# A two-layer trunk on one core: the attention's output product in plain fp32, and five places of split weights lent to the experts' weights

## The chip, the cores and the metric

The kernel runs on one core of a Trainium2 chip. The metric is the device time of one execution in microseconds (us), median of several runs. One execution is also profiled; its times are read below.

## The reference

The input is 256 positions of 1024 channels. Layer 0 is a gated short convolution and a dense SwiGLU. Layer 1 is an attention over 15 heads of 64 and a mixture of 8 experts, of which each position takes 2. Cut to what matters here:

```python
def dilated_attention_mixer(h, positions, w_qkv, w_o):
    ...                                    # 3 groups of 5 heads, softmax over the groups too
    return o.reshape(b, s, ATTN_WIDTH) @ w_o          # (256 x 960) @ (960 x 1024)

def moe_swiglu(h, w_router, w_gate, w_up, w_down):
    ...                                    # gates: top 2 of 8, softmax
    for e in range(N_EXPERTS):
        out = out + gates[..., e:e + 1] * swiglu(h, w_gate[e], w_up[e], w_down[e])
```

An expert has three matrices of 1024 x 2816 fp32, 33 MiB together, and the eight have 264 MiB.

## The kernel before

**The stream of weights.** All weights come from HBM through one object, `Stream`, in the order in which `add_*` has listed them. An item is about 1 MiB (here called a unit). The kinds that matter: `"w"`, weights of the dense layers and of the attention, which are split on arrival into a rounded part (`whi`, by ScalarE) and a remainder (`wlo`, by VectorE, L222), each an fp32r tile of the pool `ring` (six of each); `"m"`, rows of `mod_w`, which VectorE adds up at once into `acc_ab` or `acc_g` (L287); `"r"`, raw fp32 weights, which the experts use unsplit. Each load takes a slot from `st.slots`. For `"w"` and `"m"` the slot goes back into the list as soon as the load is listed, and the next load into it waits on SyncE (SP) until the reader has finished; for `"r"` it goes back only at `done()`. SP issues all these loads in the order in which the code listed them. What `topup` lists is decided here:

```python
            kind, more = self.loaded[0][:2] if self.loaded else self.items[0][::2]
            if kind == "r":
                return bool(self.slots)
            n = len(more[1]) if kind == "w" else 0 if kind == "p" else 2
            return n + sum(len(u.tiles) for q in (self.ready, self.held) for u in q if not callable(u)) <= 2 * N_SPLIT
```

With `N_SPLIT = 3`, three units of split weights (six pairs of tiles) may be ready or held; an `"m"` counts as two tiles, a raw unit as none. Listing an `"m"` also puts its two adds into VectorE's program at that place.

**Order around the change.** The QKV products run as six passes (`n` 0 to 5) of two units each (`units[0]` to `units[11]`). The stream's list there is: `units[10]`, `late_g[0]`, `units[11]`, `late_g[1]`, the four units of `w_o`, `late_g[2]`, `late_g[3]`, then the experts' units, expert by expert. The five general slots `raw0` to `raw4` go round. In the last pass the first scores (`scores(its[0])`, `expo`, `norm`) stand before the products of `units[11]`, and ScalarE's copies of `vv` behind `expo`. Attention then runs as a pipeline of turns, one for each of ten pairs of head group and row half: scores, softmax, transposes, `values`. `values` leaves its result in PSUM; ScalarE rounds it into `oT[0]`, VectorE the remainder into `oT[1]` (tiles hTh, hTl).

**The output product.** `out_proj` multiplies with the four units of `w_o`: `rows` issues three fp32r matmuls of 512 columns for every block of 128 channels, row half and column half (xh by wh, xh by wl, xl by wh). One unit goes through both row halves first, with `attention_end` (the last turn) between them; the other three are kept and run by row half and column half, with the router's work (`mid`, `after`) in between. Then come the router, the choice and the gather, and the experts.

**The experts.** Each expert runs over groups of 32 tokens: two groups always, a third if it has more than 64 tokens, a fourth over 96 (`by_groups`). At `e == 1` all engines meet for a test (`overflow`, not taken). Slots for the experts' units beside the five general ones: `acc_ab`, `early0` (once), `tables`, `rawx`, six `ring` places of one pair `whi`, `wlo` each (2 x 512 KB), `rows`, `h`; each is added to the list when its first owner is done.

Of the kernel before, what the change touches and what calls it, by code (L numbers as in the profile page):

```python
# [10 lines left out]
F32 = mybir.dt.float32  # L11
# [3 lines left out]
AF = mybir.ActivationFunctionType  # L15
# [3 lines left out]
P = 128  # L19
D = 1024  # L20
S = 256
NT = S // P
KT = D // P
# [4 lines left out]
HD = 64  # L28
AW = NH * HD
# [12 lines left out]
N_SPLIT = 3  # L42
# [10 lines left out]
def trunk_kernel(ctx: ExitStack, tc: tile.TileContext, a, out):  # L53
    nc = tc.nc
    ve, sc, pe, gp = nc.vector, nc.scalar, nc.tensor, nc.gpsimd

    cst = ctx.enter_context(tc.tile_pool(name="cst", bufs=1))
    pers = ctx.enter_context(tc.tile_pool(name="pers", bufs=1))
    ring = ctx.enter_context(tc.tile_pool(name="ring", bufs=2 * N_SPLIT))
# [3 lines left out]
    def f32(ap):  # L63
        return ap.bitcast(F32)
# [4 lines left out]
    def tp_tile():  # L69
        return psum.tile([P, 512], F32, name="tp", tag="tp", bufs=2)  # L70

    def mm(o, l, r, start, stop):
        pe.matmul(o, l, r, start=start, stop=stop, skip_group_check=True)  # L73
# [64 lines left out]
    def part_of(raw, n, c0, c1):  # L138

        if isinstance(raw, list):  # L140
            h, c1 = c0 // 1024, c1 - c0 // 1024 * 1024
            return raw[h][:n, c0 - h * 1024:c1]
        return raw[:n, c0:c1]
# [127 lines left out]
    st = Stream()  # L271
# [131 lines left out]
    def unit(*args):  # L403
        return lambda: add_unit(*args)
# [4 lines left out]
    def mod_g(n):  # L409
        return [lambda q=q: mods[n].add_g(q) for q in range(4)]  # L410
# [6 lines left out]
    def in_order(*units):  # L417
        for u in units:
            u()
# [41 lines left out]
    w_qkv, w_o = a["attn_w_qkv"][0], a["attn_w_o"][0]  # L461
# [3 lines left out]
    late_g = mod_g(3)  # L465
    plan(units[6:10], mod_ab(3, (1,)))
    in_order(units[10], late_g[0], units[11], late_g[1])
    os = [unit(w_o, 2 * q, 2, 0, D) for q in range(3)]
    in_order(*os)

    def load_last(raw):
        nc.sync.dma_start(part_of(raw, P, 0, D), w_o[6 * P:7 * P, :])
        nc.sync.dma_start(part_of(raw, HD, D, 2 * D), w_o[7 * P:AW, :])
    st.add_w(load_last, D, [(P, 0, D), (HD, D, 2 * D)])
    in_order(*late_g[2:])

    def add_raw(w, k0, nk, c0, cw):

        pad = 1024 if nk == 2 else cw
        half = 1024 // pad  # L480

        def load(raw):
            for f, n in [(0, half), (half, nk - half)] if isinstance(raw, list) else [(0, nk)]:
                dst = part_of(raw, P, f * pad, (f + n) * pad).rearrange("p (k n) -> p k n", n=pad)[:, :, :cw]
                nc.sync.dma_start(dst, w[(k0 + f) * P:(k0 + f + n) * P, c0:c0 + cw].rearrange("(k p) n -> p k n", p=P))
        st.add_r(load, pad)

    for e in range(NE):
        for c0, cw in ROUNDS:
# [36 lines left out]
    def modulated(i, rstd, mod, hs, h=None):  # L526
# [4 lines left out]
        ve.tensor_add(h[:, c], h[:, c], mod.B[:, c])  # L531
        return h

    def split_to(hi, lo, src):
        sc.activation(hi, src, AF.Copy)  # L535
        ve.tensor_sub(lo, src, f32(hi))
# [7 lines left out]
    def new_hT():  # L544
        return (pers.tile([P, KT, S], F32R, name="hTh"), pers.tile([P, KT, S], F32R, name="hTl"))
# [24 lines left out]
    def rows(po, u, xs, first, last, cols=(0, 512)):  # L570

        n = len(xs)
        for kk, (xh, xl) in enumerate(xs):
            r = xh.shape[0]
            for c0 in cols:
                wh, wl = u.at(kk * D + c0, 512, r)
                o = po[c0 // 512]
                mm(o, xh, wh, first and kk == 0, False)
                mm(o, xh, wl, False, False)
                mm(o, xl, wh, False, last and kk == n - 1)  # L580
# [206 lines left out]
    for n in range(3):  # L787
        u = st.get(99 if n else 1)
# [20 lines left out]
    for n in range(3):  # L809
        u = st.get()  # L810
# [6 lines left out]
        if n == 1:  # L817
            t = conv_sum(0, v)
    ps = [mm_tile() for _ in range(3)]
    for n in range(3):  # L820
        for kh in range(2):
            u = st.get()
# [8 lines left out]
            if kh == 1 and n == 1:  # L831
                t = conv_sum(1, v)
# [25 lines left out]
    with tc.tile_pool(name="ffn", bufs=1) as pool:  # L858
# [5 lines left out]
        for n, (c0, cw) in enumerate(PIECES):  # L864
# [3 lines left out]
            for w, k0 in ffn_order(turns) if n == 0 else turns:  # L868
                u = st.get()
# [52 lines left out]
        r = rstd_of(1, lambda: st.finish(1))  # L922
# [9 lines left out]
    oT = None  # L932
# [30 lines left out]

    its = [(j, i) for j in range(HPG) for i in range(NT)]
    Ss, Ps, PTs = {}, {}, {}
    rests = deque()
    scale = HD ** -0.5

    def head(j, g):
        hd = order[g] * HPG + j  # L970
        return hd, slice(HD * (hd % 2), HD * (hd % 2) + HD)
# [41 lines left out]
    def values(it):  # L1013
        j, i = it
        pt = PTs.pop(it)
        n = i + 1
        p = tp_tile().rearrange("p (g t) -> p g t", g=4)
        for g in range(3):
            hd, rs_ = head(j, g)
            for b in range(n):  # L1020
                mm(p[rs_, g], vv[:, b, hd * HD:(hd + 1) * HD], pt[:, g * n + b], b == 0, b == n - 1)
        ts = slice(i * P, (i + 1) * P)
        _, rs_ = head(j, 0)
        b0 = j // 2
        hd, rs2 = head(j, 2)
        parts = ((rs_, slice(b0, b0 + 6, 5), slice(0, 2)), (rs2, hd // 2, 2))
        for r, b, g in parts:
            sc.activation(oT[0][r, b, ts], p[r, g], AF.Copy)

        def rest():  # L1030
            for r, b, g in parts:
                ve.tensor_sub(oT[1][r, b, ts], p[r, g], f32(oT[0][r, b, ts]))
        rests.append(rest)

    for n, (c0, cw) in enumerate(QKV):
        if n == 2:
# [48 lines left out]
        else:  # L1085
            for kh in range(2):
                u = st.get()
# [7 lines left out]
                        post(i)  # L1095
                st.done(0 if n == len(QKV) - 1 and kh == 1 else 99)

    def router_scale(q):
        p = mm_tile().rearrange("p (r k t) -> p r k t", r=2, k=4)
        for r, row in enumerate((mods[3].A, mods[3].B)):  # L1100
            for k in range(4):
                pe.transpose(p[:, r, k], row[:, (4 * q + k) * P:(4 * q + k + 1) * P], ident)
        sc.activation(col_a[:, 4 * q:4 * q + 4], p[:, 0, :, 0], AF.Copy)
        bT.append(pool.tile([P, 4, P], F32, name="bT", tag="rope", bufs=3))
        sc.activation(bT[q], p[:, 1], AF.Copy)
# [7 lines left out]

    bT = []
    N = len(its)
    oT = new_hT()
    def turn(n):
        if n == N:
            sc.activation(warm, eps, AF.Sqrt)
        if 0 < n < N:  # L1120
            scores(its[n])
        if 0 < n - 1 < N:
            norm(its[n - 1])
        while rests:
            rests.popleft()()
        if 0 <= n - 2 < N:
            probs(its[n - 2])
            probs_out(its[n - 2])
        if 0 < n < N:
            expo(its[n])  # L1130
        if n in (9, 10):
            router_scale(n - 9)
        if n == 11:
            st.topup()
        if n == 10:
            st.add_slot("acc_ab", lambda: pers.tile([P, 2048], F32, name="raw", tag="acc_ab"))
        if n == 12:
            router_shift()
        if 0 <= n - 3 < N:
            values(its[n - 3])  # L1140
        if n == N + 2:
            rests.popleft()()

    for n in range(N + 2):
        turn(n)
# [1 line left out]
    def attn_act(q, i):  # L1147
        r = []
        for k in (2 * q, 2 * q + 1):
            m = P if k < 7 else HD  # L1150
            r.append((oT[0][:m, k, i * P:(i + 1) * P], oT[1][:m, k, i * P:(i + 1) * P]))
        return r

    moe = hT32 = lg = pairs = sel = gates = px = None
# [1 line left out]
    def attention_end():  # L1156

        nonlocal moe, hT32, lg, pairs, sel, gates, px
        turn(N + 2)
        attn.close()  # L1160
        moe = ctx.enter_context(tc.tile_pool(name="moe", bufs=1))

        st.add_slot("early0", lambda: moe.tile([P, 2048], F32, name="early0", tag="acts"), once=True)
        st.add_slot("tables", lambda: [pers.tile([P, 1024], F32, name="rawt", tag="tables"),
                                       moe.tile([P, 1024], F32, name="rawm")])
        hT32 = moe.tile([P, KT, S], F32, name="hT32", tag="rawx")
        lg = moe.tile([P, NT, NE], F32, name="lg")
        pairs = moe.tile([P, NT, 2, NE, NE], F32, name="pairs", tag="xg")
        sel = moe.tile([P, NT, NE], BF16, name="sel")
        gates = moe.tile([P, NT, NE], F32, name="gates")  # L1170
        px = moe.tile([P, NT, NE], F32, name="px")
# [74 lines left out]
    def gathered(pr, ks, p, copy):  # L1246
        if pr not in xg:
            xg[pr] = moe.tile([P, KT, S], F32, name="xg", tag="xg")
        copy(xg[pr][:, ks[0]:ks[-1] + 1].rearrange("p k t -> p (k t)"), p[:, :len(ks) * S])

    def act_copy(o, i):
        sc.activation(o, i, AF.Copy)  # L1252

    def spread(e):

# [122 lines left out]
    for_router(1, 1)  # L1378
    router(1, 1, lp)
    st.add_slot("rawx", lambda: moe.tile([P, 2048], F32, name="rawx", tag="rawx"))  # L1380
    for n in range(2 * N_SPLIT):
        st.add_slot(f"ring{n}", lambda: [ring.tile([P, 1024], F32, name="rawr", tag=t) for t in ("whi", "wlo")])
    st.topup()
    rs[1] = rstd_of(1, lambda: remainder_h(0, 0))
    round_h(0, 1)
# [21 lines left out]
    rest = mm_tile()  # L1407
# [15 lines left out]
    for h in range(2):  # L1423
        r = slice(64 * h, 64 * h + 64)
# [100 lines left out]
    _, n_all = nc.values_load_multi_w_load_instructions(counts[0:1, :], engines=[mybir.EngineType.PE], min_val=0, max_val=S)  # L1525
    for e in range(NE):
        pr, b = divmod(e, 2)
# [9 lines left out]
        for r, (c0, cw) in enumerate(ROUNDS):  # L1537
            bank = groups()
            N = cw // 2
# [88 lines left out]
    r = moe.tile([P, NT], F32, name="r")  # L1628
    t = moe.tile([P, NT], F32, name="t")
# [7 lines left out]
    last = cols[-1].start  # L1637
# [35 lines left out]
```

## Time and profile before

| | |
|---|---|
| median of 3 runs | 1189.1 us (1188.94 to 1191.66) |
| the profiled execution's own time | 1189.74 us |
| its span | 1188.1 us, 20567 instructions |
| busy TensorE (PE) / its weight loads (PEld) | 1102.9 / 614.1 us |
| busy VectorE (DVE) / ScalarE (ACT) | 549.9 / 320.3 us |
| bytes read from HBM | 395.45 MB |

Times in the rows are from the span's start. A row of the timeline gives start, duration, engine (SPq is SP issuing a load), line, operation, out<-in, how many were merged, and in brackets the idle time before it and what ended it. L73 is the helper that records every matmul; a plain fp32 product of the source stands as two MATMUL instructions, an fp32r product as one. The granted clock (PEclk) is 1.00 at 2.4 GHz and 0.50 at 1.2 GHz. The ends of matmuls are modelled, so the distance between starts tells more than a duration.

### The profile page before, as it was taken

The numbers are of one execution on the slowest core, as the hardware profiler recorded it, in microseconds if no ns is written. First come the engines' busy times: TensorE is split into PE (matmuls) and PEld (weight loads), VectorE is DVE, ScalarE is ACT, GpSimd is POOL, SyncE is SP. The second block draws the span as 40 slices with busy tenths as digits, with TensorE's granted clock in tenths as the row PEclk, the third lists the DMA queues.
The fourth block names the chain that finished last, engine by engine and source line by source line (L and its number), as shares of the span: only waits on it lengthen the run. The fifth ranks groups of instructions, "written<-read, shape, count | busy, mean of one in ns | idle before, by whom it ended". The sixth has DMA issues, their size and how long they took to land. (4 is left out here: it accounts for less than half of the span.)

```text
span 1188.1 us, 20567 instructions
## 1 busy us (share of the span) xinstructions
PE 1102.9 (93%) x8658; PEld 614.1 (52%) x8658; DVE 549.9 (46%) x863; ACT 320.3 (27%) x517; POOL 29.6 (2%) x45
## 2 busy tenths in 40 slices
PE   5999999999999999997989999999999999998986
PEld 1899699997878776332323233333333333332233
DVE  3599798887789867321312211221221222321224
ACT  3345444454354473310201110110111021110111
POOL 2000110000001000000000000000000000000000
PEclk9999999999999999998999999999999999998999
DMA  9888797887937915999999999999779999999994
GB/s 339 303 311 330 244 330 288 294 293 283 344 103 276 333 47 192 407 406 408 403 408 408 392 406 408 347 394 400 267 298 404 401 383 408 406 405 408 406 372 156
DMA packets 139400, 398.40 MB, mean 335 GB/s; under 512 B 11299, under 2 KB 22331, under 8 KB 139274
## 3 DMA queue, kind: packets, MB, share of 16 engines
q1 hardware_dynamic: 138698, 396.47, 87.7%
q8 instruction: 101, 1.65, 0.6%
q14 instruction: 25, 0.20, 0.0%
q0 software_dynamic: 576, 0.07, 0.0%
HBM read 395.45 MB, written 1.05 MB: 334 GB/s over the span
## 5 line engine op out<-in xcount | busy, mean ns | idle before, releaser
L73 PE MATMUL mm<-raw,xg 128*32 128x512 f32 (+1 forms) x1616 | 245.8, 570 | 19.1 <-DVEq L1531 7.1
L73 PE MATMUL mm<-rawr,xg 128*32 128x512 f32 (+1 forms) x1360 | 166.7, 559 | 9.2 <-PEq L1435 4.1
L222 DVE TENSOR_TENSOR wlo<-raw,whi 128x1024 fp32r<-128x1024 f32 (+2 forms) x130 | 153.8, 1221 | 27.5 <-ACT whi L220 26.6
L220 ACT ACTIVATE whi<-raw 128x1024 fp32r<-128x1024 f32 (+2 forms) x130 | 132.1, 1045 | 117.3 <-PE mm L73 77.6
L1442 DVE TENSOR_TENSOR gu<-gu,mm 64x512 f32<-64x512 f32 (+1 forms) x96 | 62.0, 646 | 217.2 <-ACT gu L1441 216.7
L73 PE MATMUL mm<-hTh,whi 128*128 128x256 f32 x544 | 150.2, 291 | 1.4 <-ACT hTh L535 1.4
L73 PE MATMUL mm<-hTh,wlo 128*128 128x256 f32 x544 | 146.8, 283 | 0.8 <-DVE wlo L222 0.8
L73 PE MATMUL mm<-hTl,whi 128*128 128x256 f32 x544 | 147.2, 284 | 0.0
L73 PEld LDWEIGHTS mm<-raw,xg 128*32 128x32 f32 x1616 | 70.8, 111 | 130.0 <-issue 103.0
L1441 ACT ACTIVATE gu<-mm 64x512 f32<-64x512 f32 (+1 forms) x96 | 51.5, 551 | 306.0 <-PE mm L73 190.5
L73 PEld LDWEIGHTS mm<-rawr,xg 128*32 128x32 f32 x1360 | 53.3, 110 | 102.4 <-issue 84.8
L73 PEld LDWEIGHTS mm<-hTh,whi 128*128 128x128 f32 x544 | 102.7, 196 | 3.9 <-ACT hTh L535 2.1
L73 PEld LDWEIGHTS mm<-hTl,whi 128*128 128x128 f32 x544 | 101.2, 192 | 2.9 <-issue 1.4
L73 PEld LDWEIGHTS mm<-hTh,wlo 128*128 128x128 f32 x544 | 101.2, 192 | 1.0 <-DVE wlo L222 1.0
L73 PE MATMUL mm<-raw,acts 128*32 128x512 f32 (+1 forms) x784 | 86.3, 562 | 10.7 <-DMA raw<-in_moe_w_down_dram 7.7
L73 PE MATMUL mm<-rawr,acts 128*32 128x512 f32 x608 | 73.2, 595 | 3.6 <-PEq L1433 2.0
L1453 DVE COPY acts<-tp 128x256 f32<-128x256 f32 (+1 forms) x48 | 19.2, 400 | 90.1 <-ACT acts L1252 89.8
L73 PEld LDWEIGHTS mm<-raw,acts 128*32 128x32 f32 x784 | 26.1, 109 | 64.3 <-issue 50.7
L287 DVE SCALAR_TENSOR_TENSOR acc_ab<-raw,csil,acc_ab 128x1024 f32<-128x1024 f32 x40 | 51.2, 1281 | 6.1 <-DMA acc_ab<-in_mod_b_dram 5.4
L73 PE MATMUL mm<-whi,hTh 128*128 128x512 f32 (+1 forms) x128 | 50.1, 409 | 0.7 <-ACT hTh L535 0.7
L1499 DVE TENSOR_TENSOR og<-mm,G 128x512 f32<-128x512 f32 x14 | 9.0, 685 | 89.4 <-PEq L1435 51.7
L73 PE MATMUL mm<-rawx,xg 128*32 128x512 f32 (+1 forms) x224 | 47.9, 561 | 0.8 <-PEq L1435 0.5
(268 smaller groups left out, 1328.9 us busy)
## 6 DMA issues: line engine op xcount, KB each, us to landing
raw<-in_moe_w_down_dram SPq DMA_DIRECT2D x36, 1024.0 KB, 12.7
rawr<-in_moe_w_down_dram SPq DMA_DIRECT2D x66, 512.0 KB, 10.0
raw<-in_mod_w_dram SPq DMA_DIRECT2D x64, 512.0 KB, 5.2
raw<-in_moe_w_gate_dram SPq DMA_DIRECT2D x29, 1024.0 KB, 14.2
raw<-in_moe_w_up_dram SPq DMA_DIRECT2D x27, 1024.0 KB, 13.1
rawr<-in_moe_w_up_dram SPq DMA_DIRECT2D x48, 512.0 KB, 10.4
rawr<-in_moe_w_gate_dram SPq DMA_DIRECT2D x48, 512.0 KB, 10.2
raw<-in_mod_w_dram SPq DMA_DIRECT2D x16, 1024.0 KB, 6.4
```

The lines of the kernel that those rows point to most:

```text
L73: pe.matmul(o, l, r, start=start, stop=stop, skip_group_check=True)
L220: sc.activation(hi[:n, :c1 - c0], src, AF.Copy)
L222: ve.tensor_sub(lo_, src, f32(hi)))
L287: ve.scalar_tensor_tensor(acc, w, csil[:, k:k + 1], acc, op0=OP.mult, op1=OP.add)
L1441: sc.activation(a[64:, :N], bank[g][:64, :N], AF.Silu)
L1442: ve.tensor_mul(a[64 * g:64 * g + 64, :N], a[64:, :N], bank[g][64:, :N])
L1453: copy(acts[:, 8 * r:8 * r + 2 * nb, g:g + 32].rearrange("p (j m) t -> p m j t", j=2), v[:, :, n])
L1499: ve.tensor_mul(og[:, g - 1], bank[g], G2)
```

## The change

`w_o` is loaded as raw fp32 (`"r"`) and not split; `oT` is one fp32 tile, copied from PSUM half by ScalarE and half by VectorE; `rows` issues one fp32 matmul in place of three. `late_g[2]` and `late_g[3]` keep their place in the list behind `w_o`. After the QKV passes five ring places become slots, and for each free slot a load is listed without being used yet; the sixth is added in `attention_end`, and the adding of all six after the output product goes.

```diff
     in_order(units[10], late_g[0], units[11], late_g[1])
-    os = [unit(w_o, 2 * q, 2, 0, D) for q in range(3)]
-    in_order(*os)
-
-    def load_last(raw):
-        nc.sync.dma_start(part_of(raw, P, 0, D), w_o[6 * P:7 * P, :])
-        nc.sync.dma_start(part_of(raw, HD, D, 2 * D), w_o[7 * P:AW, :])
-    st.add_w(load_last, D, [(P, 0, D), (HD, D, 2 * D)])
-    in_order(*late_g[2:])
...
+    for q in range(3):
+        add_raw(w_o, 2 * q, 2, 0, D)
+
+    def load_last(raw):
+        nc.sync.dma_start(part_of(raw, P, 0, D), w_o[6 * P:7 * P, :])
+        nc.sync.dma_start(part_of(raw, HD, D, 2 * D), w_o[7 * P:AW, :])
+    st.add_r(load_last, D)
+    in_order(*late_g[2:])
...
             for c0 in cols:
+                if isinstance(u, RawUnit):
+                    mm(po[c0 // 512], xh, u.at(kk, c0, 512)[:r], first and kk == 0, last and kk == n - 1)
+                    continue
...
-        for r, b, g in parts:
-            sc.activation(oT[0][r, b, ts], p[r, g], AF.Copy)
-
-        def rest():
-            for r, b, g in parts:
-                ve.tensor_sub(oT[1][r, b, ts], p[r, g], f32(oT[0][r, b, ts]))
-        rests.append(rest)
+        for copy, (r, b, g) in zip((act_copy, ve.tensor_copy), parts):
+            copy(oT[r, b, ts], p[r, g])
...
+    def add_split_slots(ns):
+        for n in ns:
+            st.add_slot(f"ring{n}", lambda: [ring.tile([P, 1024], F32, name="rawr", tag=t) for t in ("whi", "wlo")])
+
+    add_split_slots(range(2 * N_SPLIT - 1))
+    for _ in range(len(st.slots)):
+        st.load()
...
-    oT = new_hT()
+    oT = pers.tile([P, KT, S], F32, name="oT", tag="hTh")
...
-        while rests:
-            rests.popleft()()
...
-        if n == N + 2:
-            rests.popleft()()
...
-            r.append((oT[0][:m, k, i * P:(i + 1) * P], oT[1][:m, k, i * P:(i + 1) * P]))
+            r.append((oT[:m, k, i * P:(i + 1) * P], None))
...
+        add_split_slots((2 * N_SPLIT - 1,))
...
-    for n in range(2 * N_SPLIT):
-        st.add_slot(f"ring{n}", lambda: [ring.tile([P, 1024], F32, name="rawr", tag=t) for t in ("whi", "wlo")])
```

## Rows read from the trace of the kernel before

**Rows 1.** Stretches: start:end, length, busy by engine (instructions), PEclk, DMA share, GB/s.
```profile
416.00:441.00 25.00, 24.51 (x200) 19.27 (x198) 18.02 (x49) 20.87 (x49) 0.00 (x0) 1.00 0.02 7
455.00:472.00 17.00, 15.70 (x89) 12.23 (x88) 12.37 (x30) 6.91 (x16) 0.00 (x0) 1.00 0.25 96
...
840.00:860.00 20.00, 19.02 (x160) 6.51 (x156) 5.25 (x8) 1.18 (x2) 0.00 (x0) 1.00 0.71 265
...
1080.00:1100.00 20.00, 16.55 (x100) 3.97 (x92) 4.64 (x7) 2.35 (x4) 0.00 (x0) 0.83 1.03 408
```

**Rows 2.** Timeline of DVE: the first work after an expert's last product.
```profile
544.61 1.29 DVE L1499 TENSOR_TENSOR og<-mm,G 128x512 f32<-128x512 f32 x2 [12.40 <-PEq L1433]
...
632.02 1.29 DVE L1499 TENSOR_TENSOR og<-mm,G 128x512 f32<-128x512 f32 x2 [4.09 <-PEq L1433]
...
936.16 1.29 DVE L1499 TENSOR_TENSOR og<-mm,G 128x512 f32<-128x512 f32 x2 [22.51 <-PEq L1435]
...
1007.84 1.29 DVE L1499 TENSOR_TENSOR og<-mm,G 128x512 f32<-128x512 f32 x2 [4.09 <-PEq L1433]
```

**Rows 3.** Timeline of PE where experts 0 and 1 begin (the latter after the meeting).
```profile
481.45 4.06 PE L73 MATMUL mm<-raw,xg 128*32 128x512 f32 x34 [1.24 <-ACT G L1425]
...
551.60 1.07 PE L73 MATMUL mm<-raw,xg 128*32 128x512 f32 x2 [7.14 <-DVEq L1531]
```

**Rows 4.** Stretch of low clock behind that meeting, columns as in the first group.
```profile
551.60:557.50 5.90, 5.90 (x28) 1.38 (x32) 0.00 (x0) 0.00 (x0) 0.00 (x0) 0.50 1.02 409
```

**Rows 5.** Timeline of SP's loads, from the output weights to the experts' ninth unit.
```profile
392.82 4.89 SPq L281 DMA_DIRECT2D raw<-in_attn_w_o_dram  x3
...
401.86 2.64 SPq L359 DMA_DIRECT2D raw<-in_mod_w_dram  x2
408.30 0.37 SPq L485 DMA_DIRECT2D raw<-in_moe_w_gate_dram  x1
...
440.81 0.37 SPq L485 DMA_DIRECT2D raw<-in_moe_w_gate_dram  x1
...
454.70 0.37 SPq L485 DMA_DIRECT2D raw<-in_moe_w_up_dram  x1
472.17 0.37 SPq L485 DMA_DIRECT2D rawx<-in_moe_w_gate_dram  x1
```

**Rows 6.** Timeline of DVE from the add of `late_g[1]` to the first scores.
```profile
399.24 2.60 DVE L287 SCALAR_TENSOR_TENSOR acc_g<-raw,csil,acc_g 128x1024 f32<-128x1024 f32 x2
...
404.02 0.68 DVE L379 SCALAR_TENSOR_TENSOR rows<-tp,gb 128x512 f32<-128x512 f32 x1
...
408.19 0.55 DVE L983 CUSTOM_DVE_ANT_0 s<-mm,tables 128x384 f32<-128x384 f32 x1
```

**Rows 7.** Issue to landing: the load issued at 401.86, at 440.81, all of L359.
```profile
DMA to landing us min/median/max: 8.0/8.0/8.0
...
DMA to landing us min/median/max: 5.2/5.2/5.2
...
DMA to landing us min/median/max: 5.1/6.4/9.0
```

**Rows 8.** Timeline of ACT and PE: what stands behind the first scores.
```profile
409.40 0.52 ACT L1061 ACTIVATE vv<-mm 128x448 f32<-128x448 f32 x1
...
411.55 1.35 PE L73 MATMUL mm<-kT,qT 64*128 64x256 f32 x12
```

**Rows 9.** Timeline of PE: the same twelve `values` instructions at two clocks.
```profile
418.23 1.14 PE L73 MATMUL tp<-pt,vv 128*64 128x128 f32 x12
...
441.56 1.98 PE L73 MATMUL tp<-pt,vv 128*64 128x128 f32 x12 [0.72 <-DVE hTl L1032]
```

**Rows 10.** Timeline of PE: two fp32 products and the next; first and last of 23 fp32r.
```profile
120.10 1.88 PE L73 MATMUL tp<-acc_g,ones 128*128 128x512 f32 x4
121.41 0.79 PE L73 MATMUL mm<-whi,zh 128*128 128x512 f32 x1
...
445.18 0.39 PE L73 MATMUL mm<-wlo,hTh 128*128 128x512 f32 x1
...
450.17 0.39 PE L73 MATMUL mm<-whi,hTl 128*128 128x512 f32 x1
```

More of the change, by code (lines that the diff above doesn't have):

```diff
@@ L532, in modulated, with act_copy @@
         return h
+    def act_copy(o, i):
+        sc.activation(o, i, AF.Copy)
     def split_to(hi, lo, src):
@@ L965, in trunk_kernel @@
     Ss, Ps, PTs = {}, {}, {}
-    rests = deque()
     scale = HD ** -0.5
@@ L1249, in gathered @@
         copy(xg[pr][:, ks[0]:ks[-1] + 1].rearrange("p k t -> p (k t)"), p[:, :len(ks) * S])
-    def act_copy(o, i):
-        sc.activation(o, i, AF.Copy)
     def spread(e):
```

## The prediction, made before the change was run

> **What bounds the kernel now.** I read the page's forty slices first: the DMA runs near 400 GB/s through the experts' half of the span, with two holes ahead of it and one dip inside it. The stretches put numbers on them [rows 1]: 7 GB/s while attention runs, 96 GB/s in the output product, and 265 GB/s at 840 to 860 us (the next 20 us are alike), while late, at 1080 to 1100 us, it is 408 GB/s again. So the experts' half has three parts. Near its end the weights come too slowly and set the end. In the dip the DMA has filled all places and waits for PE to free them, so PE sets the time there. In the first two experts the ends of the experts tell [rows 2]: expert 1 takes 632.02 - 544.61 = 87.4 us, expert 5, with the same two groups and the same gather inside it, 1007.84 - 936.16 = 71.7 us. Of the 15.7 us more, 7.1 are the meeting of the engines [rows 3] and 5.9/2 = 2.95 the half clock behind it [rows 4]; the other 5.7 us are waits for weights. From this follows the rule by which I count: a PE that reaches the dip later by X makes places free later by X, and the full-rate stream behind the dip ends later by X. Weights that come earlier are worth only what they save PE ahead of the dip, at most those 5.7 us.
>
> **How the stream's list runs now.** SP issues the three full units of `w_o` from 392.82, the two `late_g` loads from 401.86, the experts' first unit at 408.30, and then waits until 440.81 for the slot of a `w_o` unit that is split only in turn 11 [rows 5]. Eight experts' units are issued by 454.70, the ninth follows at 472.17, when the output product is over.
>
> **The hold on VectorE.** This is the costly part, and the diff doesn't name it. Now, when `units[9]` is done, `topup` adds `late_g[1]` (the add from 399.24 to 401.84 [rows 6]), lists the first split of `w_o`, and stops, because three split units stand ready. `late_g[2]` and `late_g[3]` are listed long after. With `w_o` raw, its four units count no tiles and are listed at once, taking four of the five slots; `units[10]` and `units[11]` count four tiles, two more are allowed, so `late_g[2]` and `late_g[3]` are listed too, at the same place, both into the one slot left, that of `late_g[1]`. So VectorE's next instructions are their adds, ahead of the row of L379 and of the first scores at 408.19 [rows 6]. The load of `late_g[2]` is issued when the slot is free, at 401.86 as now [rows 5]; the second must wait until the first is added. The landing took 8.0 us for the load issued at 401.86 and 5.2 us for one into an idle queue; L359's lie between 5.1 and 9.0 [rows 7]. I take 8.0 and 5.2: 401.86 + 8.0 = 409.9, add 2.6, 412.5, issue and landing 417.7, add 420.3, L379 0.68, scores 0.55, so the first scores end at 421.5 instead of 408.7. What is queued behind: ScalarE has `expo` and then the copies of `vv`; the first copy now ends at 409.92, 1.18 us after the scores' end, and PE's next scores need the PSUM tile that it frees. They start at 411.55 now [rows 8], and at 421.5 + 1.2 = 422.7 then. Attention is late by 11.2 us. With both landings at 5.1 it is 8.1, with both at 9.0 15.9 us.
>
> The Trainium skill's page "DMA: Bandwidth & Descriptors", section "Anatomy of one DMA — SWDGE (gpsimd) path", fits a load as 2.0 us plus bytes at 436 GB/s, an estimate of 4.4 us for 1 MiB. By it the hold would be 6.7 us and the forecast 4.5 us lower; no load of L359 here was below 5.1 us, so the rows are kept.
>
> PE then has stood idle for some 11 us. After 7.1 us idle [rows 3] it ran 5.9 us at granted 0.50, which is 1.2 GHz [rows 4]. Twelve `values` instructions took 1.14 us at full and 1.98 us at low clock [rows 9], so 0.84/1.98 of 5.9 us, 2.5 us, would be lost; the bounds are 0 and 2.95, and I take 2.0, as not all of a turn is PE's.
>
> **The output product.** 32 places (8 blocks, 2 row halves, 2 column halves) have three fp32r matmuls now. Their starts are (450.17 - 445.18)/22 = 0.227 us apart [rows 10], so 0.680 us a place. An fp32 product of the same shape stands in the trace as two instructions: two products start at 120.10, and the next fp32r matmul, issued at 121.41, shows 0.79 us instead of 0.39, so it got the array at 121.81 [rows 10]. That is 1.71/2 = 0.855 us a product. By the starts alone it would be 1.31/2 = 0.655. The ends are modelled, but the 0.40 us of queueing is in the row, so I take 0.855: 32 x 0.175 = +5.6 us, the other end being -0.8. PE is without a gap in this part and the router behind it starts from the last product, so this is on the path. Nothing comes back from the removed splits of ScalarE and VectorE, since PE hides them, but for one wait: the last `values` waits 0.72 us for a VectorE that is late by a split [rows 9]; -0.7 us. The two copies of `oT` replace two roundings and two subtractions in each turn and are hidden under PE, which is busy 24.5 of 25 us in attention [rows 1].
>
> **The five places.** Their loads stand in SP's queue behind the first expert unit, which now takes `late_g[3]`'s slot. They are held until 420.3 too, and then six units and a seventh (into `acc_ab`) come during attention at about 2.57 us a unit (1.049 MB at 408 GB/s [rows 1]), some 18 us, done before attention ends. Four more follow in the output product (`early0`, `tables`, the sixth ring place, the first freed `w_o` slot). There are 17 places in all by the code's list; all are filled when the first expert begins, and the next is freed when its first four units are used up, 64 instructions at 34 in 4.06 us [rows 3], 7.6 us later. At the same point before, 489.1, the stream has 8 + (489.1 - 472.17)/2.57 = 14.6 units [rows 3, 5]. The lead is 2.4 units, 6.2 us: enough for the 5.7 us of waits in expert 1, and no more than that is to be had. So -5.7 us, with 0 and -6.2 as bounds.
>
> **Sum.** 11.2 + 2.0 + 5.6 - 0.7 - 5.7 = +12.4 us. On the profiled execution's 1189.74 us this is 1202.1; that execution is 0.6 above the median, so I forecast 1201.5 us for the median.
>
> **Rivals.** *No hold on VectorE*: the two `late_g` adds are listed later than I read, or their data are there in time. For it: now no add of L287 near there waits, since loads run 6 us or more ahead. Against: the slot itself is freed only at 401.84. It decides if the second add ends before 408.2. Then 5.6 - 0.7 - 5.7 = -0.8, 1188.3 us, no change; with the low end of the product as well, 1182.
>
> *The product costs nothing*: at 0.655 us a place it is -0.8 instead of +5.6, so 1195. For it the starts, against it the queued matmul [rows 10].
>
> *The earlier weights bring nothing*, as the waits in expert 1 come from the order of landings and not from the lead: no -5.7, so 1207. The change would then not do what its places are for.
>
> *Attention stays at the low clock.* At 0.84/1.14 more of 24.5 us it costs 18 instead of 2.0 us, 1217.5. Against it: once at full clock, attention held 1.00 [rows 1]; no row shows it coming back from low. The Trainium skill's page "TensorE: Matmul & The Clock Gate", section "HAM oscillation — how this bites in real kernels", tells of a kernel that fell back to the low rate at every wait; no run here shows that yet.
>
> **How the numbers follow.** Forecast 0.68, no hold 0.13, cheap product 0.08, no gain from the places 0.06, low clock 0.05. Under the forecast alone the bounds give 8.1 + 0 + 5.6 - 0.7 - 6.2 = +6.8 to 15.9 + 2.95 + 5.6 - 0.7 - 5 = +18.8, 1196 to 1208. To leave out no more than 2 in 10 the range goes down to the case without a hold and up past the bounds by a little: 1187 to 1209. A measurement of this kernel can tell about 0.3%, 3.6 us, from no change. Faster by more needs no hold and a cheap product together: 0.07; within it 0.11, most of the case without a hold; slower 0.82.
>
> **What would show it.** In the trace after: two adds of L287 behind that of 399.24, each with idle time before it that a DMA ends, and the first L983 near 421; PE idle some 11 us ahead of its second scores, then a granted clock of 0.50 for about 6 us; the experts' second to seventh unit issued from 420 on; 64 fp32 instructions in the output product at 0.43 us each; expert 0 beginning at about 481.45 + 18.1 = 499.5; expert 1 about 5.7 us shorter; and the experts behind it unchanged in length. The prediction is wrong if the first scores come before 412, if the product's part is not longer, or if the dip in the DMA is gone, since then the end would follow the bytes and not PE.

## The result, and the profile after

The changed kernel takes 1201.63 us (median of 4 runs, 1199.3 to 1207.15) beside 1189.69 us for the kernel before on the same chip (4 runs, 1188.94 to 1191.66): a ratio of 1.0101, with an interval of 1.0081 to 1.0121. The profiled execution took 1201.99 us, its span is 1200.3 us against 1188.1.

The page after, its busy times and two lines of the forty slices (granted clock in tenths, GB/s):

```profile
PE 1108.1 (92%) x8626; PEld 607.1 (51%) x8626; DVE 536.6 (45%) x845; ACT 310.2 (26%) x499; POOL 29.9 (2%) x45
...
PEclk9999999999999989998999999999999999999999
...
GB/s 336 311 315 327 227 332 289 292 275 284 339 126 285 230 245 143 245 375 407 406 405 408 405 408 408 383 353 406 307 267 393 407 380 407 407 405 408 406 373 153
```

PE's busy time grew by 5.2 us, the span by 12.2, so more than half of the loss is time in which PE waits. The dip of the DMA near 860 us is still there (310 GB/s from 840 to 860 us, below), so the rule of the prediction can be used: what PE is late at the first expert, less what the earlier weights save, is what the end is late.

VectorE's timeline after, at the place of [rows 6], and then ScalarE's:

```profile
400.23 2.60 DVE L287 SCALAR_TENSOR_TENSOR acc_g<-raw,csil,acc_g 128x1024 f32<-128x1024 f32 x2
410.95 2.61 DVE L287 SCALAR_TENSOR_TENSOR acc_g<-raw,csil,acc_g 128x1024 f32<-128x1024 f32 x2 [8.12 <-DMA raw<-in_mod_w_dram]
418.37 2.60 DVE L287 SCALAR_TENSOR_TENSOR acc_g<-raw,csil,acc_g 128x1024 f32<-128x1024 f32 x2 [4.82 <-DMA raw<-in_mod_w_dram]
420.89 0.68 DVE L379 SCALAR_TENSOR_TENSOR rows<-tp,gb 128x512 f32<-128x512 f32 x1
421.49 0.55 DVE L989 CUSTOM_DVE_ANT_0 s<-mm,tables 128x384 f32<-128x384 f32 x1
...
422.70 0.96 ACT L1062 ACTIVATE vv<-mm 128x448 f32<-128x448 f32 x2
```

Each row of L287 is the pair of adds of one `late_g` item, called one add here. Two such rows stand behind that of `late_g[1]`, each with idle time that a DMA ends, and the row of L379 and the first scores stand behind them: scores at 421.49 instead of 408.19, and ScalarE's copies of `vv` after them, at 422.70.

PE's timeline after, from the second scores to the first expert:

```profile
422.11 2.50 PE L73 MATMUL mm<-kT,qT 64*128 64x256 f32 x12 [9.50 <-DVE mx L989]
...
431.32 1.15 PE L73 MATMUL tp<-pt,vv 128*64 128x128 f32 x12
...
449.30 3.70 PE L73 MATMUL mm<-raw,oT 128*128 128x512 f32 x8
452.84 1.85 PE L73 MATMUL tp<-rw,bT 128*128 128x8 f32 x16
454.62 1.14 PE L73 MATMUL tp<-pt,vv 128*64 128x128 f32 x12
455.69 18.22 PE L73 MATMUL mm<-raw,oT 128*128 128x512 f32 x40
...
484.35 1.06 PE L73 MATMUL tp<-rw,hT 128*128 128x8 f32 x8
...
497.88 0.62 PE L73 MATMUL mm<-raw,xg 128*32 128x512 f32 x2 [1.38 <-ACT G L1427]
```

PE is idle for 9.50 us; the twelve score products behind it take 2.50 us, where [rows 8] show 1.35. Stretches of the kernel after (columns as in [rows 1]):

```profile
422.10:428.80 6.70, 6.70 (x27) 4.84 (x27) 4.15 (x12) 3.56 (x9) 0.00 (x0) 0.50 0.99 377
455.00:472.00 17.00, 17.00 (x47) 7.13 (x46) 3.08 (x6) 1.33 (x4) 0.00 (x0) 1.00 0.64 248
840.00:860.00 20.00, 18.91 (x170) 7.81 (x164) 5.33 (x8) 2.35 (x4) 0.00 (x0) 1.00 0.80 310
```

The granted clock is 0.50 (1.2 GHz) for 6.7 us behind the idle time, and 1.00 later in attention. In the output product the DMA now moves 248 GB/s instead of 96.

SP's loads after, to be held against [rows 5], and VectorE's first work after experts 0, 1, 4 and 5, against [rows 2]:

```profile
402.86 11.10 SPq L359 DMA_DIRECT2D raw<-in_mod_w_dram  x2
421.00 0.37 SPq L477 DMA_DIRECT2D raw<-in_moe_w_gate_dram  x1
...
429.86 0.38 SPq L477 DMA_DIRECT2D raw<-in_moe_w_gate_dram  x1
455.84 0.38 SPq L477 DMA_DIRECT2D early<-in_moe_w_up_dram  x1
...
493.48 1.09 SPq L477 DMA_DIRECT2D rawh<-in_moe_w_gate_dram  x2
505.09 0.38 SPq L477 DMA_DIRECT2D raw<-in_moe_w_up_dram  x1
```

```profile
561.00 1.29 DVE L1501 TENSOR_TENSOR og<-mm,G 128x512 f32<-128x512 f32 x2 [12.35 <-PEq L1435]
...
643.78 1.29 DVE L1501 TENSOR_TENSOR og<-mm,G 128x512 f32<-128x512 f32 x2 [4.09 <-PEq L1435]
...
947.49 1.29 DVE L1501 TENSOR_TENSOR og<-mm,G 128x512 f32<-128x512 f32 x2 [22.52 <-PEq L1437]
...
1019.22 1.29 DVE L1501 TENSOR_TENSOR og<-mm,G 128x512 f32<-128x512 f32 x2 [4.09 <-PEq L1435]
```

The experts' first unit leaves at 421.00 instead of 408.30, the next six in attention; SP stops between 493.48 and 505.09 because all places are full. Expert 1 takes 643.78 - 561.00 = 82.8 us instead of 87.4, expert 5 71.7 as before. Some rows of the kernel before that were not shown yet, its timeline of PE in the output product, and a stretch of it:

```profile
436.14 0.50 PE L73 MATMUL mm<-whi,hTh 128*128 128x512 f32 x1
...
438.99 1.84 PE L73 MATMUL tp<-rw,bT 128*128 128x8 f32 x16
...
443.47 0.80 PE L73 MATMUL mm<-whi,hTh 128*128 128x512 f32 x1
...
444.92 0.43 PE L73 MATMUL mm<-whi,hTh 128*128 128x512 f32 x1
...
468.05 1.06 PE L73 MATMUL tp<-rw,hT 128*128 128x8 f32 x8
```

```profile
441.56:445.00 3.44, 3.44 (x16) 2.82 (x17) 0.98 (x4) 0.65 (x2) 0.00 (x0) 0.50 0.91 296
```

With them, one event after another, the loss can be followed through the kernel:

| start of | before | after | late by |
|---|---|---|---|
| add of `late_g[1]` | 399.24 | 400.23 | 1.0 |
| second scores on PE | 411.55 | 422.11 | 10.6 |
| twelve `values` of an early turn | 418.23 | 431.32 | 13.1 |
| first product of `w_o` | 436.14 | 449.30 | 13.2 |
| router's products behind the first unit | 438.99 | 452.84 | 13.9 |
| last `values` | 441.56 | 454.62 | 13.1 |
| next product of `w_o` | 443.47 | 455.69 | 12.2 |
| router's products behind the last unit, first group | 468.05 | 484.35 | 16.3 |
| expert 0 | 481.45 | 497.88 | 16.4 |
| end of expert 0 | 544.61 | 561.00 | 16.4 |
| end of expert 1 | 632.02 | 643.78 | 11.8 |
| end of expert 5 | 1007.84 | 1019.22 | 11.4 |
| end of the span | 1188.1 | 1200.3 | 12.2 |

### The profile page after: what moved, and what is told of

Read it like the earlier page. It is cut to its first block, busy times and chain, and to the rows that moved or that the text cites. A ratio compares the mean times of both kernels' runs of the same rounds, so it can differ in the third digit from the quotient of the medians.

```text
span 1200.3 us, 20445 instructions
## 1 busy us (share of the span) xinstructions
PE 1108.1 (92%) x8626; PEld 607.1 (51%) x8626; DVE 536.6 (45%) x845; ACT 310.2 (26%) x499; POOL 29.9 (2%) x45
## 3 DMA queue, kind: packets, MB, share of 16 engines
q1 hardware_dynamic: 138778, 396.47, 87.1%
## 5 line engine op out<-in xcount | busy, mean ns | idle before, releaser
L73 PE MATMUL mm<-raw,xg 128*32 128x512 f32 (+1 forms) x1576 | 257.0, 560 | 11.5 <-DMA raw<-in_moe_w_up_dram 3.9
L73 PE MATMUL mm<-rawr,xg 128*32 128x512 f32 (+1 forms) x1416 | 199.8, 566 | 17.0 <-DVEq L1533 7.1
L222 DVE TENSOR_TENSOR wlo<-raw,whi 128x1024 fp32r<-128x1024 f32 (+1 forms) x122 | 144.3, 1221 | 24.5 <-ACT whi L220 23.8
L220 ACT ACTIVATE whi<-raw 128x1024 fp32r<-128x1024 f32 (+1 forms) x122 | 123.8, 1044 | 113.1 <-PE mm L73 71.4
L73 PEld LDWEIGHTS mm<-raw,xg 128*32 128x32 f32 x1576 | 74.3, 109 | 118.6 <-issue 97.5
L73 PEld LDWEIGHTS mm<-rawr,xg 128*32 128x32 f32 x1416 | 58.1, 111 | 118.4 <-issue 90.6
L73 PEld LDWEIGHTS mm<-hTh,wlo 128*128 128x128 f32 x544 | 101.3, 192 | 1.0 <-DVE wlo L222 1.0
L73 PE MATMUL mm<-rawr,acts 128*32 128x512 f32 (+1 forms) x648 | 73.1, 555 | 4.6 <-PEq L1437 2.2
L1455 DVE COPY acts<-tp 128x256 f32<-128x256 f32 (+1 forms) x48 | 19.2, 400 | 87.4 <-ACT acts L536 87.2
L287 DVE SCALAR_TENSOR_TENSOR acc_ab<-raw,csil,acc_ab 128x1024 f32<-128x1024 f32 x40 | 51.2, 1281 | 5.9 <-DMA acc_ab<-in_mod_b_dram 5.2
L73 PEld LDWEIGHTS mm<-rawr,acts 128*32 128x32 f32 x648 | 22.4, 109 | 49.8 <-issue 42.4
L287 DVE SCALAR_TENSOR_TENSOR acc_g<-raw,csil,acc_g 128x1024 f32<-128x1024 f32 x32 | 41.0, 1281 | 13.5 <-DMA raw<-in_mod_w_dram 12.9
## 6 DMA issues: line engine op xcount, KB each, us to landing
rawr<-in_moe_w_down_dram SPq DMA_DIRECT2D x57, 512.0 KB, 11.4
rawr<-in_moe_w_up_dram SPq DMA_DIRECT2D x50, 512.0 KB, 11.4
rawr<-in_moe_w_gate_dram SPq DMA_DIRECT2D x46, 512.0 KB, 10.6
```

Source lines behind the costliest of these rows:

```text
L220: sc.activation(hi[:n, :c1 - c0], src, AF.Copy)
L222: ve.tensor_sub(lo_, src, f32(hi)))
L287: ve.scalar_tensor_tensor(acc, w, csil[:, k:k + 1], acc, op0=OP.mult, op1=OP.add)
L1455: copy(acts[:, 8 * r:8 * r + 2 * nb, g:g + 32].rearrange("p (j m) t -> p m j t", j=2), v[:, :, n])
```

## The experiments

The theory is the prediction's: a hold of two adds on VectorE, low clock behind it, a dearer product on the path, and a lead worth at most what expert 1 waits. The rivals are its rivals. The hold, the product and the places are each taken out or dosed by itself; the clock and the wait that goes are read from the traces. The first four kernels ran on one chip beside a kernel before of 1190.19 us (19 runs), the last three beside one of 1191.21 (18 runs).

**Both adds listed ahead of `w_o`.** The rest of the change stays.

```diff
-    in_order(units[10], late_g[0], units[11], late_g[1])
+    in_order(units[10], late_g[0], units[11], *late_g[1:])
...
-    in_order(*late_g[2:])
```

> Edit: in the stream's list late_g[2] and late_g[3] stand ahead of the four units of w_o, nothing else. Their loads then go into other slots, free by 395 us, and the adds find their data. Theory (VectorE is held by these two adds): the first scores come at about 409 instead of 421.5 us, PE has no idle time of 9.5 us and no stretch at half clock, expert 0 begins at about 485 instead of 497.9 us, and the time falls by 9.6 + 2.5 = 12 us to about 1189.5. Rival (the fp32 product is the main loss): the time stays above 1196.

Measured: 1190.17 us (11 runs), ratio 1.0006 (0.9996 to 1.0015). VectorE's timeline and PE's of this kernel:

```profile
399.53 7.89 DVE L287 SCALAR_TENSOR_TENSOR acc_g<-raw,csil,acc_g 128x1024 f32<-128x1024 f32 x6
...
407.93 0.55 DVE L988 CUSTOM_DVE_ANT_0 s<-mm,tables 128x384 f32<-128x384 f32 x1
...
411.85 1.35 PE L73 MATMUL mm<-kT,qT 64*128 64x256 f32 x12
```

The adds of all three items run without a gap, because their data are there; the first scores are not late, and PE's next ones by 0.3 us. The whole loss is gone: 0.0101 - 0.0006 = 0.95%, 11.3 us, hung on where two items stand in a list.

**One add ahead, one behind**, a half dose of the hold.

```diff
-    in_order(units[10], late_g[0], units[11], late_g[1])
+    in_order(units[10], late_g[0], units[11], *late_g[1:3])
...
-    in_order(*late_g[2:])
+    in_order(late_g[3])
```

> Edit: only late_g[2] is moved ahead of w_o; late_g[3] keeps its place behind it. Theory: one load is still late. It is issued at about 404.5 us behind the last unit of w_o, lands about 8 us later, and the first scores come at about 416; PE is idle for 4 to 5 us instead of 9.5. Time 1194.5 to 1197, in between. Rival (the place of the adds does not matter): as the changed kernel, 1201.6.

Measured: 1196.74 us, ratio 1.0063 (1.0047 to 1.0078). Its timeline of VectorE, of PE, and a stretch:

```profile
413.65 2.60 DVE L287 SCALAR_TENSOR_TENSOR acc_g<-raw,csil,acc_g 128x1024 f32<-128x1024 f32 x2 [9.10 <-DMA raw<-in_mod_w_dram]
416.77 0.55 DVE L989 CUSTOM_DVE_ANT_0 s<-mm,tables 128x384 f32<-128x384 f32 x1
...
417.38 2.50 PE L73 MATMUL mm<-kT,qT 64*128 64x256 f32 x12 [5.68 <-DVE mx L989]
```

```profile
417.40:421.00 3.60, 3.60 (x17) 2.87 (x19) 2.09 (x6) 2.03 (x5) 0.00 (x0) 0.50 0.94 329
```

One wait is left and costs 0.57%, where two cost 0.95%; PE's idle time is 5.68 us, more than the 4 to 5 expected. Against the kernel with both adds ahead, PE's second scores are 5.53 us late and expert 0 (491.48 against 484.98) 6.50, so the clock adds 1.0; with two adds the same differences are 10.26 and 12.90, so 2.6.

**No places: the ring places become slots only after the output product**, and the listing of a load for each free slot goes with them, once with the hold and once without.

```diff
-    add_split_slots(range(2 * N_SPLIT - 1))
-    for _ in range(len(st.slots)):
-        st.load()
...
-        add_split_slots((2 * N_SPLIT - 1,))
...
+    add_split_slots(range(2 * N_SPLIT))
```

> Edit: the six ring places are added where they were before, after the output product; the early loads go, all else is as in the changed kernel. Theory: the hold stays, and the waits for weights in expert 1 come back: expert 1 takes 87 instead of 82.8 us, time 1201.6 + 4.6 = 1206. Rival (the lead is worth nothing, or the loads in attention cost something): 1201.6 or less.

> Both edits: the adds ahead of w_o, and the six places where they were before. What is left of the change is the fp32 product on unsplit weights. Theory: product +4.8 us, the wait at the last values and the low clock behind it -1.6, nothing from places: about 1192 to 1194, 4 to 5 above the run with the adds first and the places. Rival (the product costs nothing on the path): 1188.

Measured: 1206.17 us with the hold, ratio 1.0140 (1.0123 to 1.0158); 1193.88 us without it, ratio 1.0029 (1.0019 to 1.0039). So the places are worth 0.39% with the hold (4.6 us, by ratios to different runs of the kernel before) and 3.7 us without it. By the experts it is expert 1: 87.1 and 87.0 us without places, 82.8 and 83.5 with them, while experts 0 and 2 to 5 differ by at most 0.2 us. Expert 0 begins 1.1 and 1.9 us later without places; 1.0 and 0.6 of it stand ahead of PE's second scores. The other 1.3 us of the 1.9 stand at the router's end, at a lower clock. PE's row of the router's last products in the kernel with the adds ahead and no places reads

```profile
475.66 1.87 PE L73 MATMUL tp<-rw,hT 128*128 128x8 f32 x8 [0.69 <-ACT hT L1184]
```

and stands at a granted clock of 0.50 (from 473.8 to 477.6 us). With the adds ahead and the places, the same products behind the same waits (0.61 and 0.69 us) take 1.06 us at 1.00. Why the clock fell in one and not in the other is shown by no run. SP's rows of the kernel with the adds ahead and no places show that there is no lead:

```profile
408.75 0.37 SPq L477 DMA_DIRECT2D raw<-in_moe_w_up_dram  x1
443.70 0.37 SPq L477 DMA_DIRECT2D early<-in_moe_w_gate_dram  x1
```

**More fp32 products on the path.** To the kernel with both adds ahead, each of the 16 groups of `rows` gets one more product, with a tile of zeros, which leaves the sums as they are.

```diff
+    nil = cst.tile([P, P], F32, name="nil")
+    ve.memset(nil, 0.0)
...
                     mm(po[c0 // 512], xh, u.at(kk, c0, 512)[:r], first and kk == 0, last and kk == n - 1)
+                    if kk == 0:
+                        mm(po[c0 // 512], nil[:r], u.at(kk, c0, 512)[:r], False, False)
```

> On the kernel with the adds first: after the first of a unit's two blocks, each place of the output product gets one more fp32 product with zeros as the stationary operand, 16 in all, which add nothing to the result. Theory (PE's path sets the end, an fp32 product of 512 columns costs 0.855 us, and what is late at the first expert is late at the end): the part and the first expert are 16 x 0.855 = 13.7 us later, the time about 13 us more than with the adds first, near 1203. Rival (two thirds of it hidden, or the end follows the bytes): under 1196.

Measured: 1205.25 us, ratio 1.0120 (1.0105 to 1.0134), 1.14% or 13.6 us above the kernel without them, by ratios to different runs of the kernel before, whose intervals leave about 2 us either way. PE's timeline of it, and one row of the kernel without them under it:

```profile
437.28 1.02 PE L73 MATMUL mm<-raw,nil 128*128 128x512 f32 x2
438.13 1.02 PE L73 MATMUL mm<-raw,oT 128*128 128x512 f32 x2
...
485.10 1.06 PE L73 MATMUL tp<-rw,hT 128*128 128x8 f32 x8
```

```profile
471.61 1.06 PE L73 MATMUL tp<-rw,hT 128*128 128x8 f32 x8
```

A product takes 438.13 - 437.28 = 0.85 us from start to start; sixteen make the router 13.5 us late, and expert 0 13.57 (498.55 against 484.98). So PE's time ahead of the dip reaches the end in full, shown with a dose. In the two profiled executions the end is even 16.5 us later (spans of 1203.8 and 1187.3): expert 2 takes 101.29 us for 99.72, and the rest comes behind it; by what way is not shown.

**The cheap product kept, and some places lent all the same.** This is built on the kernel before, with split `w_o` and three fp32r products. Two units go through both row halves first instead of one, two are kept instead of three, so two pairs of the ring come free in the middle of the product and are lent at once; the router's parts move by one place.

```diff
+    while rests:
+        rests.popleft()()
...
-    out_proj(4, attn_act, after, mid, each=each, between=attention_end)
+        if q == 1:
+            add_split_slots(range(2))
+            st.topup()
+    out_proj(4, attn_act, after, lambda h, n: mid(h, n + 1), 2, each=each, between=attention_end)
...
-    for n in range(2 * N_SPLIT):
-        st.add_slot(f"ring{n}", lambda: [ring.tile([P, 1024], F32, name="rawr", tag=t) for t in ("whi", "wlo")])
+    add_split_slots(range(2, 2 * N_SPLIT))
```

> On the kernel before (w_o split, three fp32r products): two units of w_o instead of one go through both row halves first and two are kept, so that two pairs of split tiles come free early in the output product; they are lent to the experts' units then, the other four places after the product as before. Theory: two more units are loaded in the output product, expert 1 loses some 4 to 5 of its 5.7 us of waits, the shorter kept part costs about 1 us at the router as VectorE is late there: 1185 to 1187. Rival (a lead is worth nothing without the fp32 product): 1190 or more.

Measured: 1186.32 us (12 runs), ratio 0.9969 (0.9956 to 0.9981). SP's timeline of it:

```profile
457.71 0.89 SPq L485 DMA_DIRECT2D rawr<-in_moe_w_gate_dram  x2
...
472.77 0.38 SPq L485 DMA_DIRECT2D rawx<-in_moe_w_gate_dram  x1
```

Two units leave some 14 us ahead of 472.17, where the ninth left before [rows 5]. Expert 0 begins at 482.08, 0.6 us later than before, and expert 1 takes 82.11 us, 5.3 less. Expert 2 takes 100.97, 1.1 more, and the later ones together about as long as before; the span is 1184.3. This kernel beats both, the kernel before by 0.3%.

**The same with VectorE's add of the shift later**, and with it the rounding on ScalarE, both behind the last residual, so that the router's input would come with less in its way.

```diff
+        residual(i, h, po, mods[2])
+        if (i, h) == (1, 1):
+            ve.tensor_add(nxt[0], nxt[0], B)
             round_h(0, 0)
-        residual(i, h, po, mods[2])
...
-            ve.tensor_add(nxt[0], nxt[0], B)
```

> As the run before, and VectorE's add of the shift to the first row half, with its rounding on ScalarE, stands behind the last residual instead of ahead of it. Theory: the about 1 us at the router comes back: 1184 to 1186. Rival (that add is not in the way): the same as the run before.

Measured: 1187.43 us (7 runs), ratio 0.9973 (0.9960 to 0.9986): nothing is gained. PE's row of the router's last products in the kernel before, in the kernel above, and in this one:

```profile
471.04 1.06 PE L73 MATMUL tp<-rw,hT 128*128 128x8 f32 x8 [0.69 <-ACT hT L1182]
```

```profile
470.82 1.88 PE L73 MATMUL tp<-rw,hT 128*128 128x8 f32 x8 [0.69 <-ACT hT L1184]
```

```profile
471.90 1.28 PE L73 MATMUL tp<-rw,hT 128*128 128x8 f32 x8 [1.69 <-ACT hT L1184]
```

The wait for `hT` got 1.0 us longer, not shorter; that the add where it stood was in the way fell as an idea. The first two rows tell where the about 1 us at the router came from: in the kernel above these products begin 0.2 us earlier than before, behind the same wait, but take 0.8 us longer, at a granted clock of 0.50 (from 470.8 to 472.8 us). So it is the clock, and no late VectorE, by which expert 0 is late there.

## Why the prediction was right

The time came out at 1201.63 us for a forecast of 1201.5. Step by step:

**The hold** was foreseen in place and kind, and it is the loss: without it the change is neutral, with one of the two items 0.6 of the loss is left. It was taken at 11.2 us and measured 10.56 - 0.99 = 9.6, since this execution was 1.0 us late already ahead of it. The first landing was 8.0 us as taken (402.86 to the add at 410.95), the second some 0.4 shorter than 5.2. The rest is the step by which PE's next scores need the PSUM tile that the first copy of `vv` frees: they started at 422.11, ahead of that copy at 422.70, and their idle time is ended by VectorE. What freed PE was that VectorE had read the first scores (421.49 + 0.55 = 422.04), so 0.07 us stood where 1.18 was counted.

**The clock.** Taken at 2.0 us out of bounds of 0 and 2.95; measured 13.1 - 10.6 = 2.5, with 6.7 us at 0.50 instead of the 5.9 of [rows 4]. The rival in which attention stays at the low clock fell: the twelve `values` at 431.32 and at 454.62 take 1.15 and 1.14 us, the full-clock price of [rows 9]. The Trainium skill's page "TensorE: Matmul & The Clock Gate", section "HAM oscillation — how this bites in real kernels", tells of a fall at every wait; here the one long wait brought one fall, and inside attention it did not repeat.

**The product.** Its price was right and the cheap rival fell. The first four places took 2.85 us before and 3.54 after, 0.17 more each; the other 28 to the router took 24.58 and 28.66, 4.08 more. The 0.77 us by which before's three rows from 443.47 to 444.92 exceed 0.680 belongs to them too, and 0.69 + 4.08 + 0.77 = 5.5 for the 5.6 foreseen. The added products tell the same by a dose. The Trainium skill's page "FP8 and Floating Point Precision", section "TensorE Precision Notes", counts four passes for true FP32; the rows give 0.855/0.227 = 3.8 times an fp32r product, which is near it.

**The wait that goes** was mis-sized: -0.7 foreseen, -2.4 measured. The wait itself gave 0.79 us (438.99 to 441.56 against 452.84 to 454.62). But before, the low clock of [rows 9] stood behind it, 3.44 us at 0.50; after, there is neither wait nor low clock, the last `values` are 0.84 us shorter and the first three products 0.77. The prediction used that very row as a price for low clock, and did not ask whether the low clock itself would go. In all eight kernels without the wait, the kernel after and the seven of the experiments, these twelve products take 1.14 or 1.15 us. That the wait alone, and not also the thin router products ahead of it, brought the low clock was not tried; waits alike, 0.5 to 0.7 us at the router's end, have the next products at full clock in the kernel before and at low clock in two kernels of the experiments.

**The five places** were worth 4.6 us in expert 1 for the 5.7 foreseen, all of it where the prediction put it. Stretches of expert 1 behind the meeting, before and then after:

```profile
551.60:632.00 80.40, 74.28 (x613) 26.34 (x613) 16.61 (x32) 9.78 (x21) 0.00 (x0) 0.96 1.03 406
```

```profile
568.00:643.80 75.80, 71.79 (x613) 25.01 (x613) 16.64 (x33) 9.82 (x21) 0.00 (x0) 0.96 1.03 406
```

The same 613 products, and the DMA at 406 GB/s in both, so the bytes still set the pace of expert 1, and being ahead shortens it. In these stretches PE waits 4.2 us for DMA before and 2.2 after, and its weight loads, partly under running products, 12.2 and 8.4. So the waits shrank where the prediction put them, though its count, by which about 1.1 us would be left, isn't what the trace shows.

**The sum** is then 1.0 + 9.6 + 2.5 + 5.5 - 2.4 - 4.6 = 11.6 us, with 0.6 in small differences to the span's 12.2. Against the 12.4 foreseen the hold was 1.6 too high, and the wait gave 1.7 more than counted; the execution's own 1.0, the clock's 0.5, the lead's 1.1 that did not come and the small differences make up for them, so part of the closeness is luck. The range had a slip of its own: its upper sum takes 5 us off for the places, whose bound was given as 0; with 0 it would be +23.8. The same terms without hold and clock give 5.5 - 2.4 = 3.1 for expert 0 in the kernel with the adds ahead; it begins 3.5 late, 0.3 of it ahead of attention.

**What stays open.** The end is 0.8 us later than expert 5's end would have it. Expert 6 takes 77.2 us for 75.9 before, and the last expert 0.6 less than before. Both together are within 0.2 us of the kernel before in the two kernels without places, and between 0.5 less and 1.7 more in those with them; by what way is shown by no run here. Nor is it shown why expert 2 takes 101.0 to 101.3 us in the two kernels with the split product and in the one with more products, and 99.7 to 99.9 in all others.

## What to carry to other kernels

Before an item of a planned stream changes its kind, work out again what the planner then lists where: here two adds that nobody touched moved ahead of the first scores on an in-order engine, and waiting there for their data, with the low clock behind it, cost all the time lost. Earlier weights were worth what the next consumer waits for and no more, so a cheaper way to some of the places (two units kept instead of three) beat the dear way to all. When a wait is taken out, ask whether the slow clock behind it goes too, and price both.

## What the runs showed of the hardware that was not expected

Idle times of PE of 5.68, 7.14 and 9.50 us were each followed by a granted clock of 0.50, for 3.6, 5.9 and 6.7 us; the first twelve score products took 2.50 us after the shortest as after the longest, for 1.35 at full clock. Attention came back to 1.00 by itself. Short waits went either way: behind 0.61 and 0.69 us at the router's end the clock stayed at 1.00 in the kernel with the adds ahead and was 0.50 in the one that also has no places.

The load that held VectorE longest took 8.0 us from issue to landing, against 5.2 into an idle queue [rows 7]. The trace of the kernel after shows the time as three stretches, which move some 2.2 MB together, twice the load's own bytes, so others were under way with it:

```profile
402.90:405.60 2.70, 2.70 (x15) 2.51 (x14) 0.00 (x0) 0.00 (x0) 0.00 (x0) 1.00 1.03 382
405.60:407.40 1.80, 1.80 (x13) 1.38 (x11) 0.00 (x0) 0.00 (x0) 0.00 (x0) 1.00 1.02 230
407.40:410.90 3.50, 3.50 (x19) 3.19 (x18) 0.00 (x0) 0.00 (x0) 0.00 (x0) 1.00 0.54 206
```

In the middle one the DMA engines are busy throughout (1.02) at only 230 GB/s. The last piece of `w_o` has 64 rows, and so fills 64 partitions; that this piece is the cause was not tried.
